# 512 columns of weights per product in the experts' second half and the last feed-forward matrix, and an end on rows of tokens

## The chip, the cores and the metric

One core of one Trainium2 chip. A time is device microseconds of one execution; the figure compared is the median of several executions. Of the kernel before three were timed: 1426.92, 1429.77 and 1431.12 us, median 1429.77.

## The reference

One sequence of 256 tokens with 1024 features goes through two transformer blocks in fp32. What the change touches is the second half of the first block's expert layer (PEER) and the end of the second block:

```python
# first block, expert layer: 128 x 128 experts, 16 chosen per head and token, 8 heads
act = jax.nn.gelu(jnp.einsum('tkd,td->tk', ue, ht), approximate=False)   # ue = u[chosen]
out = jnp.einsum('tk,tkd->td', gt * act, ve)                             # ve = v[chosen]
x = x + out
x = rms_norm(x, norm_final_g)
...
# second block: h += hybrid_mixer(...); h += cross_attention(...); then
up = hn @ w_up
gate = jax.nn.gelu(causal_dwconv(up[..., :D_FF], conv_f_w, conv_f_b), approximate=False)
h = h + (gate * up[..., D_FF:]) @ w_down          # D_FF = 2816
return rmsnorm(h, final_g)
```

## The kernel before

*Layout.* Activations lie with features on the 128 partitions and tokens along the free axis: x is a tile of 8 x 256, feature group c and token t. The output is written in the same layout, and the host transposes it.

*Products.* Every weight matrix is cut into blocks of 128 x 1024 floats that come from HBM one after the other (512 KB each, through SyncE's queue, into the four buffers "wraw"; class Slots, L300). ScalarE casts a block to a rounded high part (`W.pre_h`, tile "wh"), VectorE subtracts to get the low part (`W.pre_l`, tile "wl"). An activation is split in the same way (names that end in H and L, or h and l). A product of the two takes three passes on TensorE: high with high, high with low, low with high. A function `slot` (L520) takes a block, runs its products, prepares the blocks that come next, and evacuates the result.

*The experts.* All 128 x 128 experts are computed densely, 128 at a time. The first half multiplies x with u, and a mask of gates, built from the chosen experts, multiplies the gelu of it. In the second half (`vslot`, L1592, 128 blocks) the rows of one block's gated activations (`parts`, L1582, split into ph and pl two blocks ahead) are multiplied with the block of v, and all blocks add up in four PSUM tiles "v" of 128 x 2 x 256 (`acc_new`, L639), features on partitions. That is `formv` (L642): a 128 x 128 piece of weights stands in TensorE and the 256 tokens move past it, 8 pieces x 3 products = 24 products per block. The last matrix of the feed-forward, w_down, uses the same `formv` for its 22 blocks, named dn0 to dn21, each two blocks after the pair ug, uv (`slot` at L2315) that gives its activation (`fah`, `fal`).

*Reading in turn.* `in_turn` (L210) gives the moving operand column 0, column n, column 1, column n + 1 and so on, where n is half of the columns; `by_two` (L215) is the same order on the output's side, where it is contiguous, and `halves` (L220) and `plain` (L227) put it back in order when the result is read. `formv` and `mm2` (L501) move tokens in turn. `form1` (L571) moves weights and reads them straight: 512 columns for the tile "hi" of the first block, 256 for the values av of the first attention and mv of the cross-attention.

*After the experts.* `finish` (L1707) adds the four PSUM tiles to x (VectorE, 8 additions of 128 x 256), takes the raw norm operand of each, and squares them on ScalarE into "sq"; between its two calls stands the first block of the memory's keys (`mk_slot`, L1742), then `stats` (L1719) sums the squares with 16 small products on TensorE.

*The end.* After dn21 VectorE adds the PSUM tiles to x, ScalarE squares, TensorE sums the squares over the partitions (`stat_mm`), ScalarE multiplies x by the gains column by column, VectorE computes the root (`rsqrt_cols`, L680), TensorE and ScalarE spread it over the rows (`rows_of`, L713), and VectorE and GpSimd multiply pairs of feature groups, each followed by an output DMA (L2348).

*The order.* Each engine runs its instructions in the order in which the program issues them (`tc.manual_schedule()`, L357). Side work is written as generators, and a model of the engines' times (class Clock, L115) decides when `step` advances one. All engine calls go through one helper, so nearly all rows of the profile bear its line, L260, and are told apart by the names of their tiles.

Of the kernel before, what the change touches and what calls it, by code (L numbers as in the profile page):

```python
# [22 lines left out]
F32 = mybir.dt.float32  # L23
# [30 lines left out]
GAP_CON, GAP_W, GAP_B1, GAP_YA, GAP_YH, GAP_MP, GAP_YL, GAP_CP, GAP_FP, GAP_KV = 160, 320, 448, 416, 384, 448, 256, 448, 448, 128  # L54
# [296 lines left out]
def build(tc, xT, memT, smalls, smalls2, w1, keysT, uT, vT, w2, outT, stop=None):  # L351
# [219 lines left out]
    def form1(a, pv, i, e, width):  # L571
# [3 lines left out]
        def mm(w):  # L575
            wh, wl = w
            for t in range(2):
                ts = slice(t * 128, (t + 1) * 128)
                for cc in range(e):
# [4 lines left out]
                    PE.matmul(pv[t], ah[:, c, ts], wh[:, ws], start=first, stop=False, skip_group_check=True)  # L584
                    PE.matmul(pv[t], al[:, c, ts], wh[:, ws], start=False, stop=False, skip_group_check=True)
                    PE.matmul(pv[t], ah[:, c, ts], wl[:, ws], start=False, stop=last, skip_group_check=True)
                if t == 0:
                    half()
            return pv
# [52 lines left out]
    def formv(acc, a, first, last):  # L642
# [13 lines left out]
        return mm  # L656

# [227 lines left out]
    def finish_out():  # L885
        drain()
        nc.sync.dma_start(outT, x)
        es.close()
# [342 lines left out]
    for i in range(4):  # L1231
# [3 lines left out]
        def ev(p):  # L1235
            for t in range(2):
                S.copy(hv[:, t], p[t])
            flags.add("hv")
            vs.put(2)
# [352 lines left out]
    def vslot(k):  # L1592
        a = P.pop(k)

        def mm(w):
            formv(acc, a, k == 0, k == NK - 1)(w)
            parts(k + 2)
# [109 lines left out]
    def finish(c0, c1):  # L1707

        def accumulate(c):
            V.tensor_tensor(x[:, c], x[:, c], halves(acc[c // 2][:, c % 2]), op=OP.add)  # L1710
# [38 lines left out]
    sq = mp.tile([128, 8, T], F32, name="sq", tag="yH")  # L1749
    finish(0, 4)  # L1750
# [108 lines left out]
    skip(mp, GAP_YL)  # L1859
    yL = mp.tile([128, 8, T], F32R, name="yL")  # L1860
# [404 lines left out]
    acc = acc_new()  # L2265
# [40 lines left out]
    for n in range(1, NFF + 1):  # L2306
# [7 lines left out]
        if n >= 2:  # L2314
            need(("ff", n - 2))  # L2315
            slot(n2(f"dn{n - 2}"), formv(acc, ap_.pop(n - 2), n == 2, False), None)
    need(("ff", NFF - 1))
    slot(n2(f"dn{NFF - 1}"), formv(acc, ap_.pop(NFF - 1), False, True), None)
    sums = Sums(np2)
    pst = stat_cols()  # L2320
    z = fp.tile([128, 8, T], F32, name="z")
    sq = fp.tile([128, 8, T], F32, name="sq")

    def square(c):
        V.tensor_tensor(x[:, c], x[:, c], halves(acc[c // 2][:, c % 2]), op=OP.add)
        S.activation(sq[:, c], x[:, c], AF.Square)

    for c in range(0, 8, 2):
        square(c)
        square(c + 1)  # L2330
        if 2 <= c:
            V.tensor_tensor(sq[:, c - 1], sq[:, c - 1], sq[:, c - 2], op=OP.add)
# [154 lines left out]
```

## Time and profile before

| | |
|---|---|
| median of three runs | 1429.77 us |
| the profiled execution | 1429.11 us, of which the span is 1427.4 us |
| mean granted clock of TensorE | 0.991 of full speed |
| TensorE busy | 1381.4 us (97%), 11904 matmul records |
| VectorE busy | 1071.3 us (75%) |
| ScalarE busy | 848.0 us (59%) |
| GpSimd busy | 183.3 us (13%) |
| read from HBM | 239.64 MB, 169 GB/s over the span |

PE is TensorE's matmul, PEld its loading of the standing operand, DVE VectorE, ACT ScalarE, POOL GpSimd, SPq SyncE's DMA queue. A row of a timeline has the start in us from the span's start, the length in us, the engine, line and operation, the output tile <- the input tiles, the form, the count of instructions drawn together, and in brackets the idle time ahead of it with what ended it. Of a product's two inputs the first is the one that moves, the second the one that stands; an output of 128x256 means that 256 columns move. Matmuls overlap: the length of one record is longer than the distance from one start to the next, so the price of a product is the distance of starts. A row of the chain of waits has start, length, engine, tile, line, and the count of instructions in a row. A row of the busy times by stretch has the stretch, its length, then for TensorE, its loads, VectorE, ScalarE and GpSimd the busy us and the count of instructions (GpSimd's is "0.00 (x0)" where it has none), the granted clock, the DMA engines' mean busy share and GB/s. A row of the groups by line has form and count | busy us, mean ns of one | idle us before, with what ended most of it.

### The profile page before, as it was taken

What the parts mean: (1) busy time and instruction counts of PE and PEld (TensorE: products, weight loads), DVE (VectorE), ACT (ScalarE), POOL (GpSimd) and SP (SyncE); (2) the same over time, 40 slices, a digit from 0 to 9 for tenths busy, and PEclk for the clock granted to TensorE, in tenths of its full rate; (3) what the DMA queues carried; (4) which work ended last, traced back from release to release, by engine and by line L of the source; (5) the groups of instructions that cost most, each with busy time, mean ns of one, the idle gap of its engine ahead of it and who ended that gap; (6) DMA issues with size and microseconds to landing.
All of it is one profiled execution on the core that took longest, in us unless ns stands there. A gap on an engine that the chain in (4) does not pass through costs nothing.

```text
span 1427.4 us, 30272 instructions
## 1 busy us (share of the span) xinstructions
PE 1381.4 (97%) x11904; PEld 1354.6 (95%) x11904; DVE 1071.3 (75%) x2137; ACT 848.0 (59%) x1617; POOL 183.3 (13%) x236
## 2 busy tenths in 40 slices
PE   8999999999999999999999999999998999999996
PEld 8789998998999999999999999999997899999996
DVE  7866679899988999965555556655699674786665
ACT  5754454445599999855554545555575554655553
POOL 6100033013400000000000112000025420310000
PEclk9999999999999999999999999999999999999998
DMA  6334554554544444455556675555532443555652
GB/s 222 128 124 134 192 198 131 193 173 163 192 149 148 149 148 149 146 186 182 196 195 198 198 267 181 201 195 195 175 121 88 162 172 110 178 185 199 205 190 78
DMA packets 66926, 242.65 MB, mean 170 GB/s; under 512 B 7632, under 2 KB 7648, under 8 KB 66656
## 3 DMA queue, kind: packets, MB, share of 16 engines
q1 hardware_dynamic: 65664, 237.01, 48.9%
q0 software_dynamic: 976, 3.69, 0.7%
q8 instruction: 94, 1.54, 0.4%
q14 instruction: 48, 0.39, 0.1%
q10 hardware_dynamic: 144, 0.03, 0.0%
HBM read 239.64 MB, written 1.05 MB: 169 GB/s over the span
## 4 chain that ended last, share of the span: by engine, by line
PE 79%; DVE 12%; POOL 3%; issue 3%; ACT 2%; DMA 0%; DVEq 0%; ACTq 0%; POOLq 0%
PE v L260 50%; PE mm L260 24%; PE aux L260 6%; DVE wl L260 4%; DVE yc L260 1%; DVE hL L260 1%; DVE x L260 1%; ACT hH L260 1%; DVE nt L260 1%; DVE eq L260 1%; POOL eq L260 0%; DVE pos L260 0%; DVE xa L260 0%; ACT wh L260 0%; POOL hL L260 0%
## 5 line engine op out<-in xcount | busy, mean ns | idle before, releaser
L260 DVE TENSOR_TENSOR wl<-wraw,wh 128x1024 fp32r<-128x1024 f32 x444 | 555.8, 1257 | 45.5 <-issue 33.2
L260 ACT CAST wh<-wraw 128x1024 fp32r<-128x1024 f32 x444 | 464.3, 1047 | 206.8 <-PE v L260 147.7
L260 PE MATMUL v<-hH,wh 128*128 128x256 f32 x2088 | 582.5, 279 | 0.8 <-ACT hH L260 0.8
L260 PE MATMUL v<-hH,wl 128*128 128x256 f32 x2088 | 576.6, 276 | 5.1 <-DVE wl L260 5.0
L260 PE MATMUL v<-hL,wh 128*128 128x256 f32 x2088 | 576.1, 276 | 1.6 <-POOL hL L260 1.4
L260 PEld LDWEIGHTS v<-hH,wl 128*128 128x128 f32 x2088 | 401.9, 192 | 7.3 <-DVE wl L260 7.2
L260 PEld LDWEIGHTS v<-hL,wh 128*128 128x128 f32 x2088 | 401.9, 192 | 2.9 <-POOL hL L260 2.7
L260 PEld LDWEIGHTS v<-hH,wh 128*128 128x128 f32 x2088 | 401.8, 192 | 1.0 <-ACT hH L260 1.0
L260 PE MATMUL mm<-hH,wh 128*128 128x256 f32 x608 | 172.8, 285 | 9.7 <-DVE au L260 4.2
L260 PE MATMUL mm<-hH,wl 128*128 128x256 f32 x608 | 168.6, 279 | 1.4 <-DVE wl L260 1.4
L260 PE MATMUL mm<-hL,wh 128*128 128x256 f32 x608 | 167.1, 279 | 2.8 <-DVE hL L260 2.0
L260 PEld LDWEIGHTS mm<-hH,wh 128*128 128x128 f32 x608 | 118.6, 195 | 13.5 <-ACT wh L260 7.5
L260 PEld LDWEIGHTS mm<-hL,wh 128*128 128x128 f32 x608 | 117.4, 195 | 3.7 <-DVE hL L260 2.4
L260 PEld LDWEIGHTS mm<-hH,wl 128*128 128x128 f32 x608 | 118.5, 195 | 2.1 <-DVE wl L260 1.8
L260 DVE TENSOR_TENSOR hL<-bigA,hH 128x256 fp32r<-128x256 f32 x72 | 31.1, 432 | 74.5 <-ACT hH L260 74.5
L260 PE MATMUL mm<-h5H,wh 128*128 128x256 f32 x280 | 77.1, 275 | 0.8 <-DVE fa L260 0.8
L260 PE MATMUL mm<-h5H,wl 128*128 128x256 f32 x280 | 77.0, 275 | 0.0
L260 PE MATMUL mm<-h5L,wh 128*128 128x256 f32 x280 | 77.0, 275 | 0.0
L260 DVE TENSOR_TENSOR hL<-bigB,hH 128x256 fp32r<-128x256 f32 x56 | 23.7, 425 | 60.6 <-ACT hH L260 60.6
L260 DVE TENSOR_TENSOR ohA<-iota,i1T 128x256 f32<-128x256 f32 x128 | 53.8, 420 | 15.2 <-PE aux L260 7.2
L260 ACT ACTIVATE ohB<-ohB,gT,ngT 128x128 f32<-128x128 f32 x126 | 62.3, 495 | 4.2
L260 ACT ACTIVATE bigA<-v 128x256 f32<-128x256 f32 (+14 forms) x72 | 25.6, 356 | 64.1 <-PE v L260 64.1
(572 smaller groups left out, 2399.0 us busy)
## 6 DMA issues: line engine op xcount, KB each, us to landing
wraw<-w_dram SPq DMA_DIRECT2D x192, 512.0 KB, 3.6
wraw<-uT_dram SPq DMA_DIRECT2D x128, 512.0 KB, 3.3
wraw<-vT_dram SPq DMA_DIRECT2D x128, 512.0 KB, 4.3
s2t<-smalls_dram POOLq DMA_DIRECT2D x6, 256.0 KB, 9.8
x<-xT_dram SPq DMA_DIRECT2D x4, 256.0 KB, 5.6
kyT<-keysT_dram POOLq DMA_DIRECT2D x1, 1024.0 KB, 7.2
xm<-memT_dram POOLq DMA_DIRECT2D x4, 256.0 KB, 6.8
outT_dram<-z SPq DMA_DIRECT2D x4, 256.0 KB, 2.7
```

Of the source, the lines that this page charges most:

```text
L260: r = f(out, *a, **k)
```

## The change

- `formr` takes the place of `formv` for the 128 blocks of v and the 22 of w_down. The activations of 128 tokens stand in TensorE, and 512 columns of the weights move past, in turn: 2 halves of the tokens x 2 halves of the columns x 3 products = 12 per block. The four PSUM tiles then hold tokens on partitions and features along the free axis.
- After the last block of v the sums are copied to SBUF (tile "rows", four copies of 128 x 512, ScalarE and VectorE in turn) and turned back by 16 transposes into PSUM tiles "turned", two in the banks "mm" and two in the banks "v"; `finish` adds from these. The first block of the memory's keys writes to a "v" bank.
- Ahead of dn0 the residual x goes into the PSUM tiles by 16 fp32 products with the identity (`stream`), which transposes it.
- The end works on rows of tokens: ScalarE squares each PSUM tile with a running sum into one column, VectorE multiplies the tile by the gains (`gz`, the gains repeated on all partitions, 512 KB loaded by GpSimd's queue at the feed-forward's start); one addition and the root give a column of factors, and two scalings each on VectorE and ScalarE, each followed by a DMA, end the program. The sums over partitions, the spreading over rows and the additions to x are gone. The host's transposition of the output changes to match.
- `form1` (hi, av, mv) reads the weights in turn too, and its results are read through `halves` and `plain`.
- The tile yL is allocated earlier, under a tag that it shares with "rows".

```diff
-def build(tc, xT, memT, smalls, smalls2, w1, keysT, uT, vT, w2, outT, stop=None):
+def build(tc, xT, memT, smalls, smalls2, gzr, w1, keysT, uT, vT, w2, outR, stop=None):
...
-                    PE.matmul(pv[t], ah[:, c, ts], wh[:, ws], start=first, stop=False, skip_group_check=True)
-                    PE.matmul(pv[t], al[:, c, ts], wh[:, ws], start=False, stop=False, skip_group_check=True)
-                    PE.matmul(pv[t], ah[:, c, ts], wl[:, ws], start=False, stop=last, skip_group_check=True)
+                    o, h, l = by_two(pv[t]), in_turn(wh[:, ws]), in_turn(wl[:, ws])
+                    PE.matmul(o, ah[:, c, ts], h, start=first, stop=False, skip_group_check=True)
+                    PE.matmul(o, al[:, c, ts], h, start=False, stop=False, skip_group_check=True)
+                    PE.matmul(o, ah[:, c, ts], l, start=False, stop=last, skip_group_check=True)
                 if t == 0:
                     half()
-            return pv
+            return [halves(p) for p in pv]
         return mm
 
...
+    def formr(acc, a, first, last):
+
+        ah, al = a
+
+        def mm(w):
+            wh, wl = w
+            for t in range(2):
+                ts = slice(t * 128, (t + 1) * 128)
+                for h in range(2):
+                    hs = slice(h * 512, (h + 1) * 512)
+                    o = by_two(flat2(acc[2 * t + h]))
+                    PE.matmul(o, ah[:, ts], in_turn(wh[:, hs]), start=first, stop=False, skip_group_check=True)
+                    PE.matmul(o, ah[:, ts], in_turn(wl[:, hs]), start=False, stop=False, skip_group_check=True)
+                    PE.matmul(o, al[:, ts], in_turn(wh[:, hs]), start=False, stop=last, skip_group_check=True)
+                if t == 0:
+                    half()
+        return mm
+
+    def flat2(p):
+        return p.rearrange("p e t -> p (e t)")
...
-            formv(acc, a, k == 0, k == NK - 1)(w)
+            formr(acc, a, k == 0, k == NK - 1)(w)
...
-            V.tensor_tensor(x[:, c], x[:, c], halves(acc[c // 2][:, c % 2]), op=OP.add)
+            V.tensor_tensor(x[:, c], x[:, c], turned[c // 2][:, c % 2], op=OP.add)
...
+    rows = mp.tile([128, 2, D], F32, name="rows", tag="yL")
+    for i in range(4):
+        t, h = divmod(i, 2)
+        dst = plain(rows[:, t, h * 512:(h + 1) * 512])
+        (V.tensor_copy if h else S.copy)(dst, halves(flat2(acc[i])))
+    turned = [ps.tile([128, 2, T], F32, name=n, bufs=b) for n, b in (("mm", None), ("mm", None), ("v", 4), ("v", 4))]
+    for t in range(2):
+        for c in range(8):
+            PE.transpose(turned[c // 2][:, c % 2, t * 128:(t + 1) * 128], rows[:, t, c * 128:(c + 1) * 128], ident)
+    paired[0] = True
     finish(0, 4)
...
-    skip(mp, GAP_YL)
-    yL = mp.tile([128, 8, T], F32R, name="yL")
+    yL = mp.tile([128, 8, T], F32R, name="yL", tag="yL")
...
+    gz = fp.tile([128, D], F32, name="gz")
+    nc.gpsimd.dma_start(gz, gzr)
+
+    acc = []
+
+    def stream(c):
+        k, n = divmod(c % 4, 2)
+        for t in range(2):
+            o = halves(flat2(acc[2 * t + c // 4]))[:, k, n * 128:(n + 1) * 128]
+            PE.matmul(o, x[:, c, t * 128:(t + 1) * 128], ident, start=c % 4 == 0, stop=False, skip_group_check=True)
...
-            slot(n2(f"dn{n - 2}"), formv(acc, ap_.pop(n - 2), n == 2, False), None)
+            if n == 2:
+                acc += acc_new()
+                for c in range(8):
+                    stream(c)
+            slot(n2(f"dn{n - 2}"), formr(acc, ap_.pop(n - 2), False, False), None)
...
-    slot(n2(f"dn{NFF - 1}"), formv(acc, ap_.pop(NFF - 1), False, True), None)
-    sums = Sums(np2)
-    pst = stat_cols()
-    z = fp.tile([128, 8, T], F32, name="z")
-    sq = fp.tile([128, 8, T], F32, name="sq")
-
-    def square(c):
-        V.tensor_tensor(x[:, c], x[:, c], halves(acc[c // 2][:, c % 2]), op=OP.add)
-        S.activation(sq[:, c], x[:, c], AF.Square)
-
-    for c in range(0, 8, 2):
-        square(c)
-        square(c + 1)
-        if 2 <= c:
-            V.tensor_tensor(sq[:, c - 1], sq[:, c - 1], sq[:, c - 2], op=OP.add)
-            stat_mm(pst, [sq[:, c - 1]], c == 2, False)
-    for c in range(6, 8):
-        stat_mm(pst, [sq[:, c]], False, c == 7)
-    if stop == "x6":
-        closing(ffx, kvx, n2x)
-        return finish_out()
-    for c in range(8):
-        S.activation(z[:, c], x[:, c], AF.Copy, scale=cs("gz", c))
+    slot(n2(f"dn{NFF - 1}"), formr(acc, ap_.pop(NFF - 1), False, True), None)
+    z = fp.tile([128, 2, D], F32, name="z")
+    junk = fp.tile([128, 512], F32, name="junk")
+    sq4 = fp.tile([128, 2, 2], F32, name="sq4")
+    for i in range(4):
+        t, h = divmod(i, 2)
+        p = halves(flat2(acc[i]))
+        S.activation(junk, flat2(acc[i]), AF.Square, accum_out=sq4[:, t, h:h + 1])
+        V.tensor_tensor(plain(z[:, t, h * 512:(h + 1) * 512]), p, plain(gz[:, h * 512:(h + 1) * 512]), op=OP.mult)
     sd = np2.tile([128, 2], F32, name="sd", bufs=2)
-    rsqrt_cols(sd, pst[:, 0:2], EPS)
-    rst = np2.tile([128, T], F32, name="std")
-    rows_of(rst, sd)
-    for c in range(0, 8, 2):
-        (G if c == 4 else V).tensor_tensor(z[:, c:c + 2], z[:, c:c + 2], rst[:, None, :].to_broadcast([128, 2, T]),
-                                           op=OP.mult)
-        nc.sync.dma_start(outT[:, c:c + 2], z[:, c:c + 2])
+    V.tensor_tensor(sd, sq4[:, :, 0], sq4[:, :, 1], op=OP.add)
+    rsqrt_cols(sd, sd, EPS, 1.0 / D)
+    for i in range(4):
+        t, h = divmod(i, 2)
+        zs = z[:, t, h * 512:(h + 1) * 512]
+        if h:
+            S.activation(zs, zs, AF.Copy, scale=sd[:, t:t + 1])
+        else:
+            V.tensor_scalar(zs, zs, sd[:, t:t + 1], None, op0=OP.mult)
+        nc.sync.dma_start(outR[:, t, h * 512:(h + 1) * 512], zs)
```

*Where the instructions stand now, first place: TensorE at the end of the experts' second half.* hH and hL are the gated activations, v the sums, hm the normed memory of the next block. Before:

```order
L260 MATMUL v<-hH,wh 128x256
L260 MATMUL v<-hH,wl 128x256
L260 MATMUL v<-hL,wh 128x256
L260 MATMUL mm<-hmH,wh 128x256
L260 MATMUL mm<-hmL,wh 128x256
L260 MATMUL mm<-hmH,wl 128x256
```

and with the change:

```order
L260 MATMUL v<-wh,hH 128x512
L260 MATMUL v<-wl,hH 128x512
L260 MATMUL v<-wh,hL 128x512
L260 MATMUL mm<-ident,rows 128x128 x4
L260 MATMUL v<-ident,rows 128x128 x4
L260 MATMUL mm<-ident,rows 128x128 x4
L260 MATMUL v<-ident,rows 128x128 x4
L260 MATMUL v<-hmH,wh 128x256
L260 MATMUL v<-hmL,wh 128x256
L260 MATMUL v<-hmH,wl 128x256
L260 MATMUL v<-hmH,wh 128x256
L260 MATMUL v<-hmL,wh 128x256
```

The 24 products of a block have become 12 of 512 columns, the 16 transposes stand between the last of them and the memory's first product, and that product writes to a bank "v" instead of "mm".

*Second place: TensorE ahead of dn0,* with fah and fal the feed-forward's activation, hH and hL the normed x, x the residual. With the change:

```order
L260 MATMUL mm<-hH,wl 128x256
L260 MATMUL v<-ident,x 128x128 x16
L260 MATMUL v<-wh,fah 128x512
L260 MATMUL v<-wl,fah 128x512
L260 MATMUL v<-wh,fal 128x512
L260 MATMUL v<-wh,fah 128x512
L260 MATMUL v<-wl,fah 128x512
L260 MATMUL v<-wh,fal 128x512
L260 MATMUL v<-wh,fah 128x512
L260 MATMUL v<-wl,fah 128x512
```

The 16 products with x stand behind the last product of a block of w_up and ahead of the first of dn0; before, the products of dn0 (`v<-fah,wh 128x256`) followed there at once.

*Third place: the end.* VectorE before, after the last low part of weights (wl):

```order
L260 TENSOR_TENSOR fal<-fa,fah 128x256
L260 TENSOR_TENSOR wl<-wraw,wh 128x1024
L260 TENSOR_TENSOR x<-x,v 128x256 x4
L260 TENSOR_TENSOR sq<-sq 128x256
L260 TENSOR_TENSOR x<-x,v 128x256 x2
L260 TENSOR_TENSOR sq<-sq 128x256
L260 TENSOR_TENSOR x<-x,v 128x256 x2
L260 TENSOR_TENSOR sq<-sq 128x256
L260 TENSOR_SCALAR rsv<-aux 128x2
L260 TENSOR_SCALAR sd<-rsv 128x2
...
L260 SCALAR_TENSOR_TENSOR sd<-rst__18019,sd 128x2
L260 TENSOR_TENSOR z<-z,std 128x512 x3
```

and with the change:

```order
L260 TENSOR_TENSOR fal<-fa,fah 128x256
L260 TENSOR_TENSOR wl<-wraw,wh 128x1024
L260 TENSOR_TENSOR z<-v,gz 128x512 x4
L260 TENSOR_TENSOR sd<-sq_16219 128x2
L260 TENSOR_SCALAR rsv<-sd 128x2
L260 TENSOR_SCALAR sd<-rsv 128x2
...
L260 SCALAR_TENSOR_TENSOR sd<-rst__16232,sd 128x2
L260 TENSOR_SCALAR z<-z,sd 128x512 x2
```

Eight additions to x and three additions of squares are replaced by four multiplications with the gains and one addition of two columns; the root has the same steps, and behind it stand two scalings by a column instead of three multiplications by a spread row. ScalarE before:

```order
L260 CAST wh<-wraw 128x1024
L260 CAST fah<-fa 128x256
L260 ACTIVATE sq<-x 128x256 x8
L260 ACTIVATE z<-x,s2t 128x256 x8
L260 COPY std<-aux 128x256
```

and with the change:

```order
L260 ACTIVATE fa<-fa 128x256
L260 CAST wh<-wraw 128x1024
L260 CAST fah<-fa 128x256
L260 ACTIVATE junk,sq_16219<-v 128x512 x4
L260 ACTIVATE z<-z,sd 128x512 x2
```

Sixteen operations of 256 columns and the copy of the spread root have become four squares of 512 columns, which read PSUM, and two scalings.

## Rows read from the trace of the kernel before

**Rows 1.** Page part 4: the chain that ended last, shares by engine
```profile
PE 79%; DVE 12%; POOL 3%; issue 3%; ACT 2%; DMA 0%; DVEq 0%; ACTq 0%; POOLq 0%
```

**Rows 2.** Windows: stretch, length, busy PE to POOL, clock, DMA share, GB/s
```profile
670.00:1016.00 346.00, 344.96 (x3082) 344.36 (x3082) 207.91 (x280) 178.83 (x275) 20.39 (x40) 1.00 0.60 201
1030.00:1160.00 130.00, 119.70 (x929) 112.64 (x929) 109.11 (x232) 79.26 (x192) 52.28 (x108) 0.99 0.38 132
1240.00:1274.00 34.00, 31.64 (x274) 30.74 (x273) 29.23 (x48) 21.70 (x36) 7.35 (x8) 1.00 0.51 176
1274.00:1413.00 139.00, 139.00 (x1247) 139.00 (x1245) 94.25 (x160) 73.94 (x105) 0.00 (x0) 1.00 0.54 180
```

**Rows 3.** Critical chain: start, length, engine, tile, line, count of records
```profile
612.49 56.29 PE v L260 x504
```

**Rows 4.** Timeline, TensorE, gates: first and last of 29 records
```profile
1030.62 0.26 PE L260 MATMUL aux<-gw,hH 128*128 128x16 f32 x1
...
1033.75 0.26 PE L260 MATMUL aux<-gw,hH 128*128 128x16 f32 x1
```

**Rows 5.** Timeline, TensorE: 4-byte products, transposes, and a record after them
```profile
1208.80 1.89 PE L260 MATMUL aux<-xpT,mv 128*128 128x256 f32 x8
...
1210.64 0.28 PE L260 MATMUL mm<-oL,wh 128*128 128x256 f32 x1
...
64.12 0.60 PE L260 MATMUL aux<-ident,sc 128*128 128x128 f32 x4
...
209.23 1.06 PE L260 MATMUL aux<-kyT,q 128*128 128x128 f32 x8
```

**Rows 6.** Timeline, TensorE: first and last of ten records of 512 columns
```profile
65.03 0.39 PE L260 MATMUL v<-wl,hH 128*128 128x512 f32 x1
...
67.09 0.40 PE L260 MATMUL v<-wl,hH 128*128 128x512 f32 x1
```

**Rows 7.** Timeline, TensorE: first and last of 35 records of 256 columns
```profile
1126.14 0.28 PE L260 MATMUL mm<-wh,hmL 128*128 128x256 f32 x1
...
1130.14 0.28 PE L260 MATMUL mm<-wl,hmH 128*128 128x256 f32 x1
```

**Rows 8.** Lines by form: three groups on VectorE and ScalarE
```profile
L260 DVE SCALAR_TENSOR_TENSOR sc<-v,bias 128x512 f32<-128x512 f32 x6 | 3.8, 680 | 0.0
...
L260 ACT COPY pT<-aux 128x512 f32<-128x512 f32 x6 | 3.5, 584 | 2.1 <-PE aux L260 2.1
...
L260 ACT ACTIVATION_READ_ACCUMULATOR tj<-hc,mu 128x1 f32 x8 | 1.5, 188 | 0.0
```

**Rows 9.** Timeline where the experts' second half ends
```profile
1014.58 0.75 DVE L260 TENSOR_TENSOR x<-x,v 128x256 f32<-128x256 f32 x2
...
1017.56 0.40 ACT L260 ACTIVATE sq<-x 128x256 f32<-128x256 f32 x1
...
1018.65 1.84 PE L260 MATMUL aux<-g4w,sq 128*128 128x2 f32 x16
```

**Rows 10.** Timeline, TensorE, at the feed-forward's start
```profile
1250.07 0.38 PE L260 MATMUL v<-fah,wh 128*128 128x256 f32 x1 [0.49 <-ACT fah L260]
...
1250.85 0.38 PE L260 MATMUL v<-fal,wh 128*128 128x256 f32 x1 [0.29 <-DVE fal L260]
...
1273.62 0.35 PE L260 MATMUL mm<-h5H,wh 128*128 128x256 f32 x1 [0.81 <-DVE fa L260]
```

**Rows 11.** Timeline of the end: last product, root, products, output issue
```profile
1412.94 0.28 PE L260 MATMUL v<-fal,wh 128*128 128x256 f32 x1
...
1416.58 0.16 DVE L260 TENSOR_SCALAR rsv<-aux 128x2 f32<-128x2 f32 x1 [1.59 <-PE aux L260]
...
1418.15 0.16 DVE L260 SCALAR_TENSOR_TENSOR sd<-rst__18019,sd 128x2 f32<-128x2 f32 x1
...
1419.50 2.96 DVE L260 TENSOR_TENSOR z<-z,std 128x512 f32<-128x512 f32 x3 [1.19 <-ACT std L260]
...
1420.22 3.03 SPq L2348 DMA_DIRECT2D outT_dram<-z  x4
```

More of the change, by code (lines that the diff above doesn't have):

```diff
@@ L53 @@
 LIMIT = 2000.0
-GAP_CON, GAP_W, GAP_B1, GAP_YA, GAP_YH, GAP_MP, GAP_YL, GAP_CP, GAP_FP, GAP_KV = 160, 320, 448, 416, 384, 448, 256, 448, 448, 128
+GAP_CON, GAP_W, GAP_B1, GAP_YA, GAP_YH, GAP_MP, GAP_CP, GAP_FP, GAP_KV = 160, 320, 448, 416, 384, 448, 448, 448, 128
 WARM = 20
@@ L886, in finish_out @@
         drain()
-        nc.sync.dma_start(outT, x)
+        nc.sync.dma_start(outR, x.rearrange("p c t -> p (c t)").rearrange("p (a b) -> p a b", a=2))
         es.close()
@@ L1236, in ev @@
             for t in range(2):
-                S.copy(hv[:, t], p[t])
+                S.copy(plain(hv[:, t]), p[t])
             flags.add("hv")
@@ L2264, in build @@
     h5 = hh
-    acc = acc_new()
+    gz = fp.tile([128, D], F32, name="gz")
[6 more added lines that the diff above has]
+            PE.matmul(o, x[:, c, t * 128:(t + 1) * 128], ident, start=c % 4 == 0, stop=False, skip_group_check=True)
     fa = {}
@@ L2396, in pack @@
     out["smalls"] = sm
+    out["gzr"] = np.ascontiguousarray(np.broadcast_to(g["final_g_2"].reshape(1, D), (128, D)).astype(np.float32))
     w = g["w_in"][0]
@@ L2480 @@
             for n, a in arrays.items()}
-    outT = nc.dram_tensor("outT_dram", (128, 8, T), F32, kind="ExternalOutput").ap()
+    outR = nc.dram_tensor("outR_dram", (128, 2, D), F32, kind="ExternalOutput").ap()
     with tile.TileContext(nc) as tc:
-        build(tc, outT=outT, **args)
+        build(tc, outR=outR, **args)
     r = run_bass_kernel_spmd(nc, [{f"{n}_dram": a for n, a in arrays.items()}], core_ids=[0])
-    got = r.results[0]["outT_dram"]
-    return np.ascontiguousarray(got.transpose(2, 1, 0).reshape(1, T, D))
+    got = r.results[0]["outR_dram"]
+    return np.ascontiguousarray(got.transpose(1, 0, 2).reshape(1, T, D))
```

## The prediction

> **What bounds the kernel now.** I read the chain that ended last first: 79% of the span is TensorE [rows 1], so a change of TensorE's work counts nearly in full wherever the chain runs over it. Then the busy times by stretch [rows 2]: while the experts' second half runs (670 to 1016 us) TensorE is busy 344.96 of 346.00 us at a granted clock of 1.00, while VectorE and ScalarE have 208 and 179 us of work and the DMAs are busy 0.60 of the time. The same holds for the feed-forward (139.00 of 139.00 us from 1274). It does not hold between 1030 and 1160, where TensorE stands 10 us, nor at the feed-forward's start (1240 to 1274), where it stands 2.4 us and VectorE is busy 29 of 34 us.
>
> What a product costs in these stages: the chain lists 504 in one piece of 56.29 us [rows 3], 111.7 ns each, 24 of them 2.68 us per block of weights. [...] What fills the 111.7 is not the columns: the gates' products move 16 and 8 columns with the same loaded 128x128 operand, and 28 intervals take 1033.75 - 1030.62 = 3.13 us, 111.8 ns each [rows 4]. So the load of the standing operand is the limit, and a product that moves twice the columns per load should get rid of it.
>
> **The change, part by part.**
>
> *Experts, 128 blocks, and the last matrix, 22 blocks.* [...] What such a product takes no row shows exactly, because the moving operand is read in turn from two halves. [...] From above, if the reading in turn itself is what fills the 111.7: 2 x 111.7 = 223 ns. Farther above: 512 columns read straight through, nine intervals in 67.09 - 65.03 = 2.06 us, 229 ns [rows 6]. I take 216, the row that also streams 512 steps with its load hidden: 12 x 216 = 2.592 us instead of 2.680, 0.088 us per block: **-11.3 us** for 128 blocks, **-1.9 us** for 22. VectorE (208 us per 128 blocks, 1.62 each), ScalarE (1.4) and the DMAs (201 GB/s would become 208) stay below 2.59 us.
>
> That reading in turn is no burden rests on 256 columns: read straight they take (1130.14 - 1126.14)/34 = 117.6 ns [rows 7], more than the load; read in turn, never more than the load's 111.7. [...]
>
> *Other products with weights moving (hi, av, mv).* They are now also read in turn: 48 of 512 columns save 229 - 216 = 13 ns each, 0.6 us, on the chain; 192 of mv save 117.6 - 111.7 = 5.9 ns, 1.1 us, nearly all in stretches where TensorE bounds; 48 of av fall into the stretch at 1050 to 1063, where TensorE waits anyhow, and count nothing. **-1.6 us** (0 to -2.0).
>
> *Turning the sums back.* After the last expert, four copies (two ScalarE, two VectorE) and 16 transposes stand on TensorE ahead of the next weights. Three quarters of the sums are complete before the last product, so three copies lie beside products. A transpose takes (0.60 - 0.28)/3 = 0.11 us (four in a row, less the 0.28 of a last record [rows 5]): 16 are 1.75 us, uncovered. The fourth copy (0.6 to 0.7 us, as the 512-column forms in [rows 8]) ends about 0.95 us after the last product, when eight to twelve transposes are through: a wait of 0 to 0.3 us. Queued behind them on VectorE are the eight additions to x. Before, they began 1.4 us ahead of the last product's end, and the four squares of the first half were done at 1017.96, 0.7 us before TensorE wanted them at 1018.65 [rows 9]. Now they begin some 1.3 us after that end, 2.7 us later against a TensorE that is 1.8 us later: the slack of 0.7 is used up, 0.2 us is lost. **+2.1 us** (1.7 to 3.5). In the next blocks and in the mixer the rest follows this shift.
>
> *The residual on TensorE.* 16 plain 4-byte products of x with the identity ahead of the first block of the last matrix: two records each, (1.06 - 0.28)/7 = 0.112 us [rows 5], so 32 x 0.112 = 3.6 us. They stand where TensorE waits for the first ready factor (0.49 and 0.29 us [rows 10]), and in the same stretch for VectorE (0.81 us at 1273.62); in all 2.4 us are idle there [rows 2]. Full cover gives 1.2, none 3.6. VectorE gets one subtraction more there (0.4 us) that GpSimd had before, and 0.5 MB more is loaded. I take **+2.2 us**, near the middle.
>
> *The end.* Before: from the start of the last product (1412.94) it takes 3.64 us of additions, squares and column sums until VectorE can start the root (1416.58), 1.73 us of root to 1418.31, 1.19 us to spread it over rows, 3 us of multiplications, which end at 1422.46; the output queue's last issue ends 0.8 us later, at 1423.25, and the span 4.15 us after that [rows 11]. After: a last product of 512 columns ends 0.4 us after its start; ScalarE squares the third and fourth quarter (584 ns for 512 columns from the accumulator plus 188 to read the sum [rows 8], 0.78 each), the fourth done 1.35 us after the start; VectorE multiplies beside it (0.68). One addition of 0.2, the same root of 1.73: 3.3 us. Then two scalings each on VectorE and ScalarE (some 0.5 and 0.7 us): 4.75 us, and with the same 0.8 and 4.15 the span ends at 9.7 us. Before it was 1427.4 - 1412.94 = 14.5: **-4.8 us** (-3.5 if the four DMAs, now closer together, delay one another; -5.6 if VectorE's scalings are faster).
>
> Sum: -11.3 - 1.9 - 1.6 + 2.1 + 2.2 - 4.8 = **-15.3 us**. The profiled execution took 1429.1 us (span 1427.4), 0.7 below the median of the runs: 1413.8 against it, **1414.5 us** as a median, 1.1% faster.
>
> **Rivals.**
> 1. *Both added pieces of TensorE work cost full price, and the end gains least*: 3.5 + 3.6 instead of 4.3, -3.5 instead of -4.8. For it: the shifted chain of additions has no slack left. Against it: 2.4 us stand idle at the feed-forward's start. 4.1 us worse: 1418.6.
> 2. *The wide read loses what the narrow one gained* (slower): the two halves now lie 256 columns apart instead of 128, and a product takes the 229 ns of the straight read. 12 x 229 = 2.748 us per block, 0.068 more than now: +10.2 us in 150 blocks where I have -13.2, and the 0.6 of hi is gone: 1414.5 + 24.0 = 1438.5. It decides from 15.3/(150 x 12) = 8.5 ns above my 216, at 224.5 ns. For it: no row shows a read in turn over 512 columns. Against it: [rows 5] against [rows 3].
> 3. *The read in turn is the limit, not the load*: 223 ns, the blocks gain nothing: 1414.5 + 13.2 = 1427.7, no change. Against it: [rows 4].
> 4. *The feed does not follow*: the experts' blocks stay at 2.68 us because casts, subtractions or DMAs set the pace: 1414.5 + 11.3 = 1425.8. Against it: the loads in [rows 2].
>
> **How the numbers follow.** The forecast (1410 to 1419) gets 0.67, rival 1 0.13 (to 1421), rival 2 0.08, rival 3 0.07, rival 4 0.05. A measurement of this kernel tells 0.3% (4.3 us) from no change, so faster means below 1425.5: forecast and rival 1, a third of rival 3 and half of rival 4, since their sums scatter too: 0.84. Slower is rival 2 alone, 0.08; the rest, 0.08, is same. The range reaches from 1408 (216 becomes 213, the residual fully covered) to 1426, which takes in rival 1 and half of rival 4 and leaves out rivals 2 and 3.
>
> **What would show it.** In the profile after: TensorE records in the experts' stretch down by half and spaced 216 ns (213 to 219), a block 2.59 us, that stretch near 335 us with the granted clock at 1.00; 16 transposes of 0.11 us ahead of the next weights, with at most 0.5 us idle there; 32 records of 0.112 us ahead of the first block of the last matrix, and the idle time of 1240 to 1274 mostly gone; mv products spaced 112 ns; about 9.7 us from the start of the last product to the end of the span. A spacing over 221 ns makes the forecast wrong; a spacing of 216 with experts' blocks still at 2.68 us means rival 4.

## The result and the profile after

The changed kernel takes 1414.26 us (median of four runs, 1413.08 to 1415.30) against 1429.65 us; the ratio is 0.9897, 95% interval 0.9879 to 0.9914. The forecast was 1414.5. The profiled execution took 1415.30 us with a span of 1413.57, so its span is 13.84 us shorter than that of before; the table splits this by the starts of the same instructions on TensorE in both traces.

| stretch | before, us | after, us | difference |
|---|---|---|---|
| start to the first product with v | 669.53 | 668.83 | -0.70 |
| experts' second half, transposes, to the memory's first product | 346.44 | 337.83 | -8.61 |
| to the gates' first product | 14.51 | 14.59 | +0.08 |
| from there to the mixer's next 72 products in one piece | 12.48 | 14.11 | +1.63 |
| to the last 36 products with the memory (hm) in one piece | 159.41 | 159.27 | -0.14 |
| to the last product ahead of dn0 | 46.94 | 46.39 | -0.55 |
| to the first product behind dn3 | 29.74 | 30.12 | +0.38 |
| to the last product of dn21 | 133.89 | 132.17 | -1.72 |
| from there to the end of the span | 14.47 | 10.26 | -4.21 |

The chain that ended last, after (start, length, engine, tile, count), with rows of the experts' first and second half:

```profile
611.78 56.29 PE v L260 x504
...
668.83 145.37 PE v L260 x672
...
875.65 129.50 PE v L260 x600
```

The first half still has 504 products in 56.29 us, as [rows 3]. In the second 672 take 145.37 us, 216.3 ns each, and 600 take 129.50, 215.8: 12 are 2.59 us per block. The busy times by stretch, after (columns as in [rows 2]: the experts' second half, the feed-forward's start, the rest of the feed-forward):

```profile
669.00:1004.00 335.00, 332.64 (x1542) 290.12 (x1543) 208.65 (x278) 178.97 (x274) 19.42 (x40) 1.00 0.66 207
1236.00:1270.00 34.00, 33.73 (x262) 32.45 (x262) 29.19 (x52) 21.66 (x36) 4.42 (x5) 1.00 0.58 178
1270.00:1403.00 133.00, 133.00 (x989) 127.12 (x988) 87.92 (x147) 70.28 (x100) 0.00 (x0) 1.00 0.56 183
```

Half the records, 1542 for 3082, and the loads no longer fill the time: PEld is busy 290 of 335 us where it was 344 of 346. The DMAs move 207 GB/s instead of 201.

Behind the last expert, after (copies, transposes, additions to x, squares, the products that sum them):

```profile
1004.78 0.38 PE L260 MATMUL v<-wh,hL 128*128 128x512 f32 x1
1004.99 0.60 PE L260 MATMUL mm<-ident,rows 128*128 128x128 f32 x4
1005.19 0.69 DVE L260 COPY rows<-v 128x512 f32<-128x512 f32 x1 [0.60 <-PE v L260]
...
1006.28 0.75 DVE L260 TENSOR_TENSOR x<-x,mm 128x256 f32<-128x256 f32 x2 [0.40 <-PE mm L260]
1006.30 0.60 PE L260 MATMUL v<-ident,rows 128*128 128x128 f32 x4
1006.66 0.36 PE L260 MATMUL v<-hmH,wh 128*128 128x256 f32 x1
...
1009.27 0.40 ACT L260 ACTIVATE sq<-x 128x256 f32<-128x256 f32 x1
...
1009.42 0.73 PE L260 MATMUL aux<-g4w,sq 128*128 128x2 f32 x6
```

The 16 transposes take 1006.66 - 1004.99 = 1.67 us and nothing waits among them; the fourth copy ends at 1005.88, 0.9 us behind the last product's slot. The squares that were 0.7 us early [rows 9] are now just in time, and TensorE loses 0.08 us up to the gates.

Ahead of dn0, after (residual, first product of dn0):

```profile
1241.13 3.74 PE L260 MATMUL v<-ident,x 128*128 128x128 f32 x32
...
1244.62 0.46 PE L260 MATMUL v<-wh,fah 128*128 128x512 f32 x1
```

The 32 records take 3.5 us, and the waits of [rows 10] (0.49, 0.29, 0.81) are gone. The end, after (VectorE, ScalarE, SyncE's queue):

```profile
1402.50 2.85 DVE L260 TENSOR_TENSOR z<-v,gz 128x512 f32<-128x512 f32 x4 [3.89 <-ACT junk L260]
...
1403.31 0.38 PE L260 MATMUL v<-wh,fal 128*128 128x512 f32 x1
...
1403.94 0.60 ACT L260 ACTIVATE junk<-v 128x512 f32<-128x512 f32 x1
1404.43 0.19 ACT L260 ACTIVATION_READ_ACCUMULATOR junk<-v 128x1 f32 x1
1405.27 0.15 DVE L260 TENSOR_TENSOR sd<-sq 128x2 f32<-128x2 f32 x1
...
1407.23 1.33 ACT L260 ACTIVATE z<-z,sd 128x512 f32<-128x512 f32 x2 [2.60 <-DVE sd L260]
...
1407.74 1.82 SPq L2383 DMA_DIRECT2D outR_dram<-z  x4
```

The last square is read out at 1404.62, 1.31 us behind the last product's start, as forecast; but the addition that opens the root starts only at 1405.27, behind VectorE's fourth multiplication (0.69 us from 1404.66). Two costs were not forecast. One is in the experts' second half (cast and low part of a block of weights, the product that waits for it):

```profile
825.75 1.04 ACT L260 CAST wh<-wraw 128x1024 fp32r<-128x1024 f32 x1 [1.12 <-DMA wraw<-vT_dram]
826.29 0.48 PE L260 MATMUL v<-wl,hH 128*128 128x512 f32 x1 [1.11 <-DVE wl L260]
```

From 824 to 830 us TensorE loses 2.1 us (by the distance of starts) to weights that come late; before it lost 0.7 there, and the longest such wait was 0.2. The other stands behind the gates. The busy times by stretch there, after:

```profile
1021.00:1024.00 3.00, 3.00 (x30) 3.00 (x28) 1.06 (x1) 1.87 (x4) 0.00 (x0) 1.00 0.53 154
1024.00:1028.00 4.00, 4.00 (x22) 4.00 (x23) 2.43 (x7) 0.00 (x0) 0.00 (x0) 0.55 0.26 100
1028.00:1032.00 4.00, 4.00 (x24) 4.00 (x24) 1.00 (x2) 3.53 (x7) 0.00 (x0) 0.60 0.38 131
```

The granted clock is at its lower level (0.50 of full speed: products of 256 columns 214 ns apart, 112 right behind it) from 1024.4 to 1031.2, 6.8 us; TensorE had been busy all the time, with the gates' products of 16 and 8 columns from 1021.25. Before, the clock was lower there too, for 3.4 us:

```profile
1032.00:1036.00 4.00, 4.00 (x34) 4.00 (x34) 1.84 (x7) 0.44 (x2) 0.00 (x0) 0.88 0.39 135
1036.00:1040.00 4.00, 4.00 (x27) 4.00 (x26) 1.79 (x3) 3.62 (x7) 0.00 (x0) 0.69 0.37 131
```

### The profile page after: what moved, and what is told of

The parts are those of the page before. It is cut to its first block, busy times and chain, and to the rows that moved or that the text cites. A ratio compares the mean times of both kernels' runs of the same rounds, so it can differ in the third digit from the quotient of the medians.

```text
span 1413.6 us, 26725 instructions
## 1 busy us (share of the span) xinstructions
PE 1368.0 (97%) x10130; PEld 1292.6 (91%) x10130; DVE 1067.9 (76%) x2133; ACT 846.9 (60%) x1612; POOL 180.3 (13%) x235
## 3 DMA queue, kind: packets, MB, share of 16 engines
q0 software_dynamic: 1120, 4.21, 0.8%
q8 instruction: 80, 1.31, 0.4%
## 4 chain that ended last, share of the span: by engine, by line
PE 78%; DVE 13%; POOL 3%; issue 3%; ACT 2%; DMA 1%; ACTq 0%; DVEq 0%; POOLq 0%; SPq 0%
PE v L260 49%; PE mm L260 24%; PE aux L260 6%; DVE wl L260 5%; DVE yc L260 1%; DVE hL L260 1%; ACT hH L260 1%; DVE x L260 1%; DMA wraw<-vT_dram 1%; POOL hL L260 1%; DVE eq L260 1%; DVE tmp L260 1%; DVE pos L260 0%; DVE il L260 0%; DVE xa L260 0%
## 5 line engine op out<-in xcount | busy, mean ns | idle before, releaser
L260 PE MATMUL v<-hH,wh 128*128 128x256 f32 x1064 | 300.8, 283 | 0.0
L260 PE MATMUL v<-hH,wl 128*128 128x256 f32 x1064 | 294.9, 277 | 3.4 <-DVE wl L260 3.4
L260 PE MATMUL v<-hL,wh 128*128 128x256 f32 x1064 | 294.3, 277 | 2.3 <-POOL hL L260 2.1
L260 PEld LDWEIGHTS v<-hH,wl 128*128 128x128 f32 x1064 | 205.3, 193 | 5.3 <-DVE wl L260 5.1
L260 PEld LDWEIGHTS v<-hL,wh 128*128 128x128 f32 x1064 | 205.4, 193 | 3.3 <-POOL hL L260 3.3
L260 PEld LDWEIGHTS v<-hH,wh 128*128 128x128 f32 x1064 | 205.5, 193 | 0.0
L260 PE MATMUL v<-wh,hH 128*128 128x512 f32 x528 | 200.8, 380 | 0.9 <-ACT hH L260 0.8
L260 PE MATMUL v<-wl,hH 128*128 128x512 f32 x528 | 200.3, 379 | 1.2 <-DVE wl L260 1.1
L260 PE MATMUL v<-wh,hL 128*128 128x512 f32 x528 | 200.2, 379 | 0.0
L260 PEld LDWEIGHTS v<-wl,hH 128*128 128x128 f32 x528 | 99.8, 189 | 15.8 <-DVE wl L260 1.9
L260 PEld LDWEIGHTS v<-wh,hH 128*128 128x128 f32 x528 | 99.8, 189 | 15.4 <-ACT hH L260 1.5
```

What stands on the lines that cost most here:

```text
L260: r = f(out, *a, **k)
```

## The experiments

Times are medians; the kernel before ran beside each group (1429.22, 1428.07 and 1430.62 us in the three groups), so the ratios compare better than the times.

**Each half alone.** First the experts alone:

```diff
-            formv(acc, a, k == 0, k == NK - 1)(w)     # v blocks only;
+            formr(acc, a, k == 0, k == NK - 1)(w)     # rows, turned as changed; form1, dn and the end as before
```

> The kernel before with the change in the experts' second half alone (512 columns of weights per product, copies and 16 transposes behind it). My theory: the 128 blocks give 128 x 0.088 = 11.3 us, the transposes take 1.7 back, and the later additions to x some 0 to 1.5: 1429.7 - 8 to -9.6, so 1420 to 1421.5 us, with products spaced 216 ns. Rival (the feed does not follow in this stage, and the time came from the end and the feed-forward): spacing 216 but blocks near 2.68 us, 1427 to 1430 us.

Measured: 1422.14 us, ratio 0.9945 (0.9930 to 0.9959), -7.1 us by the medians; products at 216 ns. The forecast of -8 to -9.6 was a little high: the waits on weights (2.2 us at 825 to 829) and the lower clock behind the gates (6.8 us long) are here too. So both are there without the other half, though each rests on one profile. Then the rest alone, without form1:

```diff
-            formr(acc, a, k == 0, k == NK - 1)(w)     # v blocks, finish and form1 as before;
+            formv(acc, a, k == 0, k == NK - 1)(w)     # dn0 to dn21, the residual and the end as changed
```

> The changed kernel with the experts and the products hi, av, mv as before: only the last matrix with its residual on TensorE and the end on rows of tokens. My theory: 22 blocks give 1.9 us, the residual costs 0.7 net, the end gives 4.2: 1429.7 - 5.4 = 1424.3 us (1423 to 1426). Rival (the residual costs its full 3.6 us wherever it stands): 1427 us.

Measured: 1423.51 us, ratio 0.9959 (0.9944 to 0.9973), -5.7 us where -5.4 was expected. The two add up to 12.8 of 15.4 us; what is left for hi, av, mv and chance is 2.6, and the intervals (2 us each) say no more of the 1.6 forecast for these.

**How the 512 columns are read.**

```diff
-                    PE.matmul(o, ah[:, ts], in_turn(wh[:, hs]), ...)   # and the two other products
+                    PE.matmul(o, ah[:, ts], wh[:, hs], ...)            # output and its readers in plain order
```

> The changed kernel with the 512 columns read straight instead of in turn in both matrices. My theory (a straight read of 512 columns is slower than the load or the columns, 229.9 ns as hi before): 13.9 ns x 12 x 150 = 25 us more than the changed kernel, 1439 us, slower than the kernel before. Rival (halving the loads is the whole gain, the way of reading does not matter): 216 ns, 1414 us.

Measured: 1435.41 us, ratio 1.0039 (1.0024 to 1.0055), slower than before. The first and the last of fifteen of its records in a row (timeline, TensorE):

```profile
699.75 0.39 PE L260 MATMUL v<-wh,hL 128*128 128x512 f32 x1
...
702.96 0.39 PE L260 MATMUL v<-wl,hH 128*128 128x512 f32 x1
```

Fourteen intervals in 3.21 us, 229 ns, as [rows 6] and not 216. So half the loads alone would have lost: 12 x 229 = 2.75 us per block against 2.68. The reading in turn carries the change. The kernel is 21 us above the changed one where 25 was expected: its profile has 0.6 us of waits on weights instead of 2.1, and the lower clock behind the gates for 3.4 us instead of 6.8, which makes that stretch 1.6 us shorter.

**Who stands, with the old width.**

```diff
-                for h in range(2):
-                    hs = slice(h * 512, (h + 1) * 512)
+                for h in range(4):
+                    hs = slice(h * 256, (h + 1) * 256)     # 24 products per block, all else as changed
```

> The changed kernel with its activations standing and tokens on rows, but 256 columns of weights per product (in turn), 24 loads per block. My theory (the load of the standing operand sets 111.7 ns): 2.68 us per block, 0.088 x 150 = 13.2 us more than the changed kernel, 1427.5 us. Rival (the gain comes from the layout, from who stands and who moves, or from what is around, not from the number of loads): 1414 to 1416 us.

Measured: 1425.92 us, ratio 0.9977 (0.9968 to 0.9987): 11.7 us above the changed kernel. Its chain:

```profile
880.52 134.00 PE v L260 x1200
```

111.7 ns, 2.68 us per block, as before with the roles exchanged. So the gain comes from half as many products, each with its load, and not from the layout. Whether the 111.7 ns are the load itself, as [rows 4] suggest, or another price that a product has whatever it moves, this does not tell apart: every product here has a load of its own (before, 11904 records of each). The 13.2 us expected became 11.7; behind the gates the clock was lower for 3.4 us only, as in r3, which is 1.6 of it. The 3.3 us by which this kernel is below the one before are not the blocks'.

**The loads of the second block's memory and constants.** In the changed kernel GpSimd issues 11 loads (ten of 256 KB, one of 16 KB) between 811 and 820 us: eight in 4.3 us, the rest behind waits of 1.41 and 0.96 us for earlier ones to land.

```diff
-    for dst, src in pieces:
-        nc.gpsimd.dma_start(dst, src)
+    for _ in range(3):
         vslot(k)
         k += 1
+    for dst, src in pieces:
+        nc.sync.dma_start(dst, src)
+        for _ in range(2):
+            vslot(k)
+            k += 1
```

> The changed kernel with the 11 loads of the second block's memory and constants (256 KB each) issued through the weights' own queue, one for every second block of the experts' second half, instead of all at once through GpSimd's queue. My theory: the waits on weights of 2.1 us at 824 to 829 us in the changed kernel come from those loads, since a block of 2.59 us leaves the weights less room; they go, 1414.3 - 2 = 1412.3 us. Rival (chance of one execution, or a limit of the weights' feed itself): waits of the same size stay in the experts' stretch, 1414 us.

Measured: 1412.29 us, ratio 0.9889 (0.9871 to 0.9907). The time is the expected one, and the trace has no wait on weights at 824 to 829, but the sum came about by luck. The memory's norm is computed later here: TensorE stands 2.2 us for its root on GpSimd, up to 909.8, where the changed kernel stands 1.1 (up to 875.2), and 0.7 us behind that the clock is at its lower level for 3.4 us (products 427 ns apart). By the distance of starts the two cost 2.8 us more than the changed kernel loses there, which is more than the waits on weights gave. What makes this profile shorter stands behind the gates: the clock stays up, and that stretch takes 10.85 us instead of 14.11.

Nor is the room that a block leaves the whole cause of the waits. r4 kept the loads on GpSimd's queue and has blocks of 2.68 us, as before, and yet it loses 1.8 us to late weights at 826 to 833, where the kernel before lost 0.7.

**The residual without cover.**

```diff
             if n == 2:
                 acc += acc_new()
+            if n == 13:                                 # ahead of dn11; dn0 now opens the sums
                 for c in range(8):
                     stream(c)
```

> The changed kernel with the 16 products of the residual with the identity in the middle of the feed-forward (ahead of dn11) instead of ahead of dn0. My theory: ahead of dn0 they stand in time in which TensorE waited anyhow and cost 0.7 us net; in the middle TensorE has no idle time, so they cost 3.6 us and the old waits of some 2.6 us ahead of dn0 come back: 1414.3 + 2.9 = 1417.2 us. Rival (they cost the same anywhere): 1414.3 us.

Measured: 1413.99 us, ratio 0.9896 (0.9877 to 0.9914): by the time no difference, against the 2.9 us I expected. The trace shows a part of them. From the last product ahead of dn0 to the last of dn21 it takes 164.10 us (1238.56 to 1402.66) against 162.29 (1241.02 to 1403.31), 1.8 more, and waits of the old kind are back (timeline, TensorE):

```profile
1239.33 0.48 PE L260 MATMUL v<-wh,fah 128*128 128x512 f32 x1 [0.50 <-ACT fah L260]
...
1248.55 0.48 PE L260 MATMUL v<-wl,fah 128*128 128x512 f32 x1 [0.43 <-DVE wl L260]
```

The third old wait (0.81 in [rows 10]) did not come back. So the cover exists, but is worth 1.8 us, not 2.9, and four runs with a spread of 2 us don't show it in the time.

**A shorter end.** In the changed program VectorE's four multiplications start 0.72 us apart (1402.50, 1403.22, 1403.94, 1404.66), each within 0.05 us after ScalarE's square of the same PSUM tile is read out (1402.47, 1403.18, 1403.90, 1404.62).

```diff
+        if i < 3:
             V.tensor_tensor(plain(z[...]), p, plain(gz[...]), op=OP.mult)
...
-    for i in range(4):
+    for i in (1, 3, 2, 0):
...
+        if i == 3:                                       # behind the root, one operation with both factors
+            V.scalar_tensor_tensor(plain(zs), halves(flat2(acc[i])), sd[:, t:t + 1], plain(gz[...]), ...)
...
+        (nc.sync if i in (3, 0) else nc.scalar).dma_start(outR[...], zs)
```

> The changed kernel with a shorter end: VectorE multiplies only three quarters by the gains ahead of the root, and takes the fourth from PSUM behind it in one operation with both factors; two of the four output DMAs are issued by ScalarE. My theory: VectorE's multiplication of a quarter waits until ScalarE has squared the same PSUM tile, so that the root starts 0.6 us later than forecast; here it starts right behind the last square: from the last product's start to the span's end 9.3 to 9.7 us instead of 10.26, 1413.7 us. Rival (the multiplications are not in the way): 10.2 us, 1414.3 us.

Measured: 1411.78 us, ratio 0.9880 (0.9862 to 0.9898). The trace:

```profile
1400.29 0.38 PE L260 MATMUL v<-wh,fal 128*128 128x512 f32 x1
...
1401.64 0.16 DVE L260 TENSOR_TENSOR sd<-sq 128x2 f32<-128x2 f32 x1
```

The root now starts 1.35 us behind the last product's start, as forecast for the changed kernel, and the span ends 1410.03 - 1400.29 = 9.74 us behind it, 0.52 less. The other 2 us of the time are not the end's: this trace is shorter already ahead of it.

**The gates spread out.**

```diff
+        def mm(w):
...
             for c in range(8):
...
+                mm2(o, w, h3, chunks=(c,))
+                for t in range(2):
...                                                      # the four gate products of chunk c
+        slot(n2("xc2"), mm, ev_xc(2))
```

> The changed kernel with the 32 gate products of 16 and 8 columns spread among the 24 products of the block behind them, instead of standing in a row. My theory: the granted clock falls to its lower level behind that row (from 1024.4 to 1031.2 us in the changed kernel, 3.4 us long in the kernel before), which takes back 1.2 us of the gain; spread out, TensorE keeps its level there, at most 3.4 us less, of which the later gates give 1 to 2.7 back: 1412 to 1414 us, granted clock 1.00 in that stretch. Rival (the lower clock has nothing to do with these products): the lower clock stays, 1414.3 us or more.

Measured: 1411.62 us, ratio 0.9878 (0.9859 to 0.9896). The busy times by stretch over the gates (1019.9 to 1026.1):

```profile
1021.00:1024.00 3.00, 3.00 (x29) 3.00 (x29) 1.90 (x3) 1.44 (x4) 0.00 (x0) 1.00 0.63 180
1024.00:1028.00 4.00, 4.00 (x38) 4.00 (x37) 2.18 (x8) 3.65 (x6) 0.00 (x0) 1.00 0.42 133
```

The lower clock is gone there, but from the memory's first product to its last 36 in one piece it takes 187.23 us instead of 187.97, only 0.7 less. The clock is lower for 3.4 us each from 1061.2, 1109.0 and 1149.9 instead, behind stretches in which TensorE stands (from 1104 to 1109 it is busy 2.5 of 5 us); how much of the gain goes back there and how much by the later gates is not shown. The median is 0.4 us below the range expected, but 1.7 of the 2.5 us by which this profile is shorter than that of the changed kernel lie ahead of the memory's first product, where the edit changes nothing. That the row of gate products brings the lower clock on is not settled by this, since the kernel with the loads moved kept the row and its clock too. None of the last four ratios (0.9878 to 0.9896) differs from the changed kernel's 0.9897 by more than their intervals (0.0018 to either side) together: what these four show is in the traces.

**The versions together, and the changed kernel again.** r9: loads moved as above, the memory's root on VectorE, the shorter end, transposes by feature halves. r10: the gates spread as well. r11: as r9, but one load per block and no delay. r12: unedited.

```diff
-        rsqrt_cols(sd, p[:, 0:2], EPS, E=G)              # in g_mem
+        rsqrt_cols(sd, p[:, 0:2], EPS)
...
-    for t in range(2):
-        for c in range(8):
+    for h in range(2):
+        for t in range(2):
+            for c in range(4 * h, 4 * h + 4):
                 PE.transpose(turned[c // 2][...], rows[...], ident)
...
-        nc.gpsimd.dma_start(dst, src)                    # r11: nothing else changes in this loop
+        nc.sync.dma_start(dst, src)
```

> The changed kernel with four edits together: the loads of the memory and the constants through the weights' queue (one per second block), the root of the memory's norm on VectorE instead of GpSimd (TensorE waited 2.2 us for it with those loads later, and the clock fell behind that wait), the shorter end, and the transposes by feature halves, so that the first additions to x can start 0.4 us earlier. My theory: waits on weights -2.0, end -0.5, transposes -0.4, the wait for the root -0.7 to -1.3: 1410.3 us, and 1407 if the clock keeps its level behind the gates, as it did with the loads moved. Rival (the waits come back in another place): 1412 to 1414 us.

> As the kernel with four edits, and the gate products spread among the products of the next block as well. My theory: the clock keeps its level behind the gates in any case, and the later gates give most of it back: 0.7 us below the four edits where those show the lower clock there, 2 us above them where they do not. Rival: no difference.

> As the kernel with four edits, but one of those loads for every block, through the weights' queue, 768 KB per block of 2.59 us, 303 GB/s. My theory (the waits come from what is asked of the DMAs at once): more waits on weights than with one for every second block, 0.5 to 2 us more. Rival (it was the second queue that hurt, not the rate): the same time as the four edits.

> The changed kernel once more, unedited, as the measure for the other runs of this call: 1414.3 us (1413 to 1415.3), waits on weights of some 2 us near 825 us, and the lower clock behind the gates for 6.5 to 6.8 us if that belongs to this program, or 3.4 us or none if it is a matter of chance.

Measured, with the ratio to the kernel before: r9 1410.20 us, 0.9873 (0.9851 to 0.9896); r10 1408.95, 0.9858 (0.9836 to 0.9879); r11 1408.22, 0.9862 (0.9839 to 0.9885); r12 1413.86, 0.9892 (0.9870 to 0.9914). All runs of r11 (1407.93 to 1411.20) lie below all of r12 (1412.42 to 1414.82), so it beats both kernels. Of the 6.4 us by which its span is below that of r12 (1406.65 against 1413.09), 3.3 stand behind the gates, where its profile has the clock up. r9 took the time expected. r10 is 1.25 us below r9, 0.7 was expected, but the intervals overlap and its profile is the longer one (span 1408.6 against 1408.0), so a gain is not shown. My expectation for r11 was wrong: one load for every block does not bring waits. The busy times by stretch around those loads, first the changed kernel, then r11:

```profile
815.00:825.00 10.00, 9.86 (x46) 8.20 (x44) 3.62 (x7) 3.33 (x6) 2.26 (x5) 1.00 1.02 392
825.00:835.00 10.00, 8.84 (x40) 7.30 (x40) 7.10 (x10) 5.41 (x8) 0.85 (x1) 1.00 0.65 205
```

```profile
815.00:825.00 10.00, 10.00 (x49) 8.74 (x48) 6.40 (x10) 4.72 (x9) 0.00 (x0) 1.00 0.82 256
825.00:835.00 10.00, 10.00 (x48) 8.77 (x47) 4.91 (x7) 5.35 (x8) 0.00 (x0) 1.00 0.89 298
```

All at once, the DMAs are full (1.02, 392 GB/s) and the weights come late: TensorE is busy 8.84 of 10 us. With the same loads one by one in the weights' own queue the DMAs move 256 to 298 GB/s, and TensorE does not wait. Whether the pace or the queue does it is open: no run spreads the loads out in GpSimd's queue. r12 repeats what the changed kernel showed: waits on weights near 825 us (0.7 and 0.5 us the longest), and the lower clock behind the gates for 6.8 us.

## Why the prediction was right, step by step

- *The product of 512 columns.* Taken at 216 ns, measured 216.3 and 215.8. The price of 111.7 ns belongs to each product with its load, whoever stands (r4), and reading in turn is no burden at 512 columns: it is the straight read that costs 13 ns more (r3: 229). The second rival and the third needed 229 and 223 ns. The 216 was read off eight records of 256 columns of a 4-byte product [rows 5], (1210.64 - 1208.80 - 0.11)/8; no run shows that such a record moves 512 steps, nor the 213 ns at the lower end of the range. What the runs showed in their place is the 215.8 to 216.3 of the wide product itself, with the loads busy 290 of 335 us.
- *Experts, -11.3.* The blocks gave 128 x (2.680 - 2.593) = 11.1 us by the chain's rows. Of the stretch, 346.44 - 3072 x 0.1117 = 3.3 us were something else before (waits, the memory's sums); after, 337.83 - 1.67 - 1536 x 0.2161 = 4.2. The 0.9 between is the price of the fourth rival in small: the feed follows all along, except where 11 other loads run beside it (2.1 us of waits on weights against 0.7). That step, "the DMAs stay below", was argued from a mean over 346 us, and the mean did not show the 10 us in which it fails.
- *The last matrix, -1.9.* 18 of the 22 blocks lie in the stretch that became 1.72 us shorter, 0.096 each, near the 0.088 taken.
- *Turning back, +2.1.* 1.67 for the transposes and 0.08 behind them: 1.75, at the lower end.
- *The residual, +2.2 (1.2 to 3.6).* Below the range: +0.38 up to dn3, and with the four blocks' 0.35 added, 0.7. The idle time that I took the cover from (2.4 us) goes by modelled ends of the products. By the distance of starts TensorE waited 29.74 - 241 x 0.1117 = 2.8 us between the last product ahead of dn0 and the end of dn3, and 0.1 is left of it.
- *The end, -4.8.* Measured -4.21: the term missed that VectorE's multiplications wait for ScalarE tile by tile, 0.6 us (r7 shows it: 1.35 us to the root, as forecast, once the fourth is out of the way).
- *hi, av, mv, -1.6.* The spacing came as forecast: hi 216 ns, mv as the two rows below show (timeline, TensorE, after; compare [rows 7]), 34 intervals in 3.79 us, 111.5 ns. hi's 48 products take 15.36 us from the first start to the last, 16.05 before: 0.69 less. That the whole stretch up to the experts is 0.70 shorter as well is luck: hi starts 2.3 us later than before and what follows it is 2.3 us shorter, and in the later runs with the same first half the first product with v starts anywhere from 666.3 to 668.9 us. Of the gain on mv, 0.5 us is given back where w_out starts, in a new wait of TensorE for a low part of weights. The sum over that stretch is -0.14, over the next -0.55; with the 0.70 that makes -1.4.

```profile
1118.47 0.28 PE L260 MATMUL mm<-wh,hmL 128*128 128x256 f32 x1
...
1122.26 0.28 PE L260 MATMUL mm<-wl,hmH 128*128 128x256 f32 x1
```

- *Not in the sum:* the longer stretch at the lower clock behind the gates, +1.6. So misses that cost (the clock, 1.6 us; the experts' stretch, 1.0; the end, 0.6; hi, av and mv, 0.2) met ones that gained (the residual with the last matrix, 1.6; turning back, 0.35), 1.5 short in all: the spans differ by 13.84 where the sum has 15.3. That the medians differ by 15.4 is luck of the sample: the profiled execution of after is the slowest of its four, 1.0 above their median, and that of before is 0.5 below its own. The main term held, half as many products at 216 ns; that 1414.5 and 1414.26 lie 0.2 us apart did not follow from the working.

## What to carry to other kernels

Where a product of 256 columns costs no more than one of 16 or 8 (111.7 and 111.8 ns here), a wider moving side is worth a trial, but the way in which it is read decides whether that pays: here 512 columns were worth 11 us in the experts read in turn, and read straight they made the whole kernel 6 us slower than before. A feed that has slack on the mean has to be looked at where other loads run beside it; here the waits went when these were put into the same queue, one by one. Let no step of a last reduction wait behind work that the result doesn't need yet.

## What the runs showed that was not expected

- The stretch at the lower clock behind the gates had three lengths in the profiles, which hold one execution of each kernel: 6.8 us in the five kernels with wide products read in turn for the experts, the loads on GpSimd's queue and the gates in a row (after, r1, r6, r7, r12), 3.4 us in before, r2, r3, r4 and r9, none in r5 and r11, with the same row of gate products in each. The length goes with the moment of the fall: 2.5 to 3.1 us behind the row's first product where it lasted 6.8 us, 4.0 to 4.7 us behind it where it lasted 3.4. From the gates' first product to those 72 in one piece it takes 14.11 us in the changed kernel, 12.48 before and 10.85 in r11. What sets that moment was not found; r9 and r11 differ only in the pace of the loads some 190 us earlier, and in when the memory's norm behind them is computed.
- r5, r9 and r11 have another 3.4 us at the lower clock between 1064 and 1071 us, right behind a stretch in which TensorE stands (in r11 it is busy 0.9 of the 3.4 us ahead of it). Up to dn0 that costs only 0.2 us in r5 and r11: TensorE stands there anyhow (in the changed kernel it is busy 15.80 of the 20 us from 1050 to 1070).
- In r5 one wait of 2.2 us of TensorE in a dense stretch was followed, 0.7 us later, by 3.4 us at the lower clock. The waits of up to 1.3 us for the same root in the other profiles were not.
